# A bidirectional encoder trunk on one core: group norm per scan step, substitution in one piece, 512-column products

## The chip, the cores and the metric

The kernel runs on one core of one Trainium2 chip. The metric is the device time of one execution in microseconds (us); several executions of the same program are taken and their median is compared. All times inside the kernel come from one execution recorded by the hardware profiler.

The engines are named as in the profile: PE is the matrix engine (PEld its weight loads), DVE the vector engine, ACT the scalar engine, POOL the general engine, SP the queue from which this kernel issues its DMAs.

## What is computed

The program is two layers of an encoder on 256 tokens of width 1024, then a final norm. Every sub-layer is scaled and shifted by nine vectors that a product of the conditioning vector with `ada_w` gives.

```python
def reference(x, c, positions, ada_w, ada_b, ...):
    cs = jax.nn.silu(c)
    for l in range(DEPTH):
        mod = cs @ ada_w[l] + ada_b[l]
        sh1, sc1, gt1, sh2, sc2, gt2, sh3, sc3, gt3 = jnp.split(mod, N_MOD, axis=-1)
        h = modulate(rmsnorm(x, norm_gains[l, 0]), sh1, sc1)
        x = x + 0.5 * gt1[:, None, :] * swiglu(h, ffn_wi[l, 0], ffn_wo[l, 0])
        h = modulate(rmsnorm(x, norm_gains[l, 1]), sh2, sc2)
        x = x + gt2[:, None, :] * hybrid_mixer(h, ...)
        h = modulate(rmsnorm(x, norm_gains[l, 2]), sh3, sc3)
        x = x + 0.5 * gt3[:, None, :] * swiglu(h, ffn_wi[l, 1], ffn_wo[l, 1])
    return rmsnorm(x, final_norm)
```

`swiglu` is a product with `ffn_wi` (1024 to 2 x 2816), a gate, and a product with `ffn_wo` (2816 to 1024). The mixer has three branches on one input projection: A and B are attentions, C is a recurrent scan (RWKV-7) that runs once forwards and once backwards, followed by a group norm per head:

```python
    _, ys = lax.scan(_rwkv_step, init, (tm(r), tm(decay), tm(k), tm(v), tm(-kk), tm(kk * a)))
    y = _flip_bwd(jnp.moveaxis(ys, 0, 2))
    mean = jnp.mean(y, axis=-1, keepdims=True)
    var = jnp.mean(jnp.square(y - mean), axis=-1, keepdims=True)
    yn = ((y - mean) * lax.rsqrt(var + GN_EPS)).reshape(2, B, S, C) * gn_w + gn_b
    ...
    return (jnp.sum(yn + bonus, axis=0) * g).astype(pr.dtype)
```

The three branch outputs are each multiplied by a gate and a branch matrix, added, and multiplied by `w_out`.

## The kernel before

**Dense products.** Activations lie with channels on the 128 partitions and the 256 tokens along the free axis. Each fp32 weight tile and each fp32 activation is split into a rounded part (hi) and the rest (lo). Weights come in by DMA as pieces of 128x1024 (`wraw`); ACT casts a 128x512 quarter to `whi` (L374), DVE subtracts it for `wlo` (L383). A ring of four such quarters (`NSPL`) feeds PE. For each 128x128 tile PE makes three matmuls of 256 columns, in `mm3`: whi with hi (L418), whi with lo (L419), wlo with hi (L420). `dense` runs `mm3` over the tiles of one output block.

**Feed-forward, second product.** 22 gated tiles `z` times `ffn_wo`, 8 output blocks `m`, in four feed-forwards: 704 weight tiles. `residual` (L609) then adds the PSUM block, scaled by the gate vector, to the residual `xT` on DVE; the next norm's work follows from it.

**The scan (branch C).** The 256 tokens are four chunks of 64. In step n the forward direction takes chunk n and the backward direction chunk 3-n, both in the same instructions. For each n, `invert` inverts a triangular matrix for all 16 heads: it starts with 8x8 blocks in `blocks8` (gathering the blocks, then a forward substitution of seven steps, two small DVE operations in each, L1288 and L1292, each of which needs the one before), spreads the result (L1295), transposes it (`flip`, L1300), and then joins blocks with matmuls `pX` and `pT`. `values` prepares the values, and `scan` makes the step: `pAS`, `pU`, `pS`, `pY`. Two threads of `invert` take (0, 2) and (1, 3); two chunks' buffers are there (`s_ck`), and a step frees one when its `pY` has been copied. One buffer of values is there (`s_vl`), freed at the same point.

**Group norm.** `post(d, t)` works on one direction and one half of the tokens (two chunks): squares on ACT, sums by matmul (`pvar`), square root on ACT, reciprocal on DVE, transposes (`pgi`), then products with the gate `G1` and sums with the other direction's result and the bonus `bon`. The halves are complete after step 1 (two of the four) and after step 3 (the other two). The last two write the branch's output `oC` (hi by ACT L1516, lo by DVE L1518), on which the branch matrix of C waits. `y` is kept in the place of the values.

**The order of the work** is written out when the program is built. Each piece of work is a thread; `yield on(engine, time, latency)` says which engine the next instructions occupy and for how long by estimate, `wait` and `take` are events and buffers. A planner (`Order.run`) always takes the thread that can start first, by priority (the lower number first) where several can start at the same time, and so fixes the order of instructions on each engine. The engines run that order as it stands. `weights_lo` has priority -1, `residual` and evacuations 0 to 2, `invert`, `scan` and `post` 3, `values` 4, the bonus (`finish`) 6, the dense stream 7, the reduction of `ada_w` (L482, `araw`) 9.

## Time and profile before

| what | value |
|---|---|
| median of 3 runs | 1536.39 us (1534.38 to 1541.68) |
| the profiled execution, its own time | 1537.14 us |
| its span, first to last instruction | 1535.3 us |
| mean granted TensorE clock | 0.99 |
| PE busy | 1495.0 us (97%) |
| PEld busy | 1424.6 us (93%) |
| DVE busy | 1283.9 us (84%) |
| ACT busy | 859.4 us (56%) |
| DMA | 315.76 MB, mean 206 GB/s |

How to read it: busy time is the time in which an engine has an instruction under way; PE's instructions overlap, and the pace of a stream is read from the starts of its instructions. The granted clock is the share of full speed at which PE was clocked in a stretch: 1.00 is 2.4 GHz and 0.50 is 1.2 GHz. In rows, `out<-in` names the tiles that an instruction writes and reads, L418 is line 418 of the kernel, and brackets give the idle time before an instruction and what ended it.

### The profile page before, as it was taken

The page shows a single profiled execution, that of the slowest core. Times are in us where ns is not written, and L with a number is a line of the kernel's source. Part 1 is how long each engine was busy: PE and PEld are TensorE (multiplying, and loading weights), DVE is VectorE, ACT ScalarE, POOL GpSimd, SP SyncE. Part 2 cuts the span into 40 slices and gives each one's busy share as a digit, 9 for nine tenths or more (in the row PEclk, how much of TensorE's full clock was granted, in tenths as well). Part 3 has the DMA queues.
Part 4 walks back from the last instruction along what each step waited for, and adds up shares of the span by engine and source line. Part 5 has one row for each costly group of instructions (what it writes and reads, how often), then busy time and mean ns, then how long its engine had stood idle before and what let it go on. Part 6 is the DMA issues. An engine that isn't in the chain of part 4 may idle for free.

```text
span 1535.3 us, 36372 instructions
## 1 busy us (share of the span) xinstructions
PE 1495.0 (97%) x14470; PEld 1424.6 (93%) x14470; DVE 1283.9 (84%) x2731; ACT 859.4 (56%) x1735; POOL 2.3 (0%) x22
## 2 busy tenths in 40 slices
PE   6999999999999989999999999999999998999998
PEld 6999999988888979999999999998888998999997
DVE  8889789989878888988789877899897888898664
ACT  4556466575444447555565545676655445665554
POOL 0000000000000000000000000000000000000000
PEclk9999999999999979999999999999999999999999
DMA  9688775525345645888668886644343456567553
GB/s 343 226 293 277 259 239 188 179 102 172 118 153 166 211 165 188 280 286 271 223 201 273 276 271 222 216 159 161 109 149 102 167 207 234 167 212 267 189 183 124
DMA packets 97377, 315.76 MB, mean 206 GB/s; under 512 B 11572, under 2 KB 23092, under 8 KB 97208
## 3 DMA queue, kind: packets, MB, share of 16 engines
q1 hardware_dynamic: 96920, 313.35, 60.8%
q8 instruction: 113, 1.85, 0.5%
q14 instruction: 56, 0.46, 0.1%
q10 hardware_dynamic: 288, 0.10, 0.0%
HBM read 310.27 MB, written 3.15 MB: 204 GB/s over the span
## 4 chain that ended last, share of the span: by engine, by line
PE 89%; DMA 5%; DVE 3%; issue 1%; SPq 1%; ACT 0%; DVEq 0%; ACTq 0%
PE pmain L418 21%; PE pmain L419 20%; PE pmain L420 20%; DMA araw<-in_ada_w_dram 3%; PE pearly L418 3%; PE pearly L420 2%; PE pearly L419 2%; DVE wlo L383 1%; PE pT L1225 1%; PE pX L1213 1%; PE pS L1568 1%; PE po L1608 1%; PE pfirst L419 1%; PE pmain L1724 1%; PE pfirst L420 1%; PE pfirst L418 1%
## 5 line engine op out<-in xcount | busy, mean ns | idle before, releaser
L374 ACT CAST whi<-wraw 128x512 fp32r<-128x512 f32 x828 | 508.1, 619 | 444.8 <-PE pmain L419 283.2
L383 DVE TENSOR_TENSOR wlo<-wraw,whi 128x512 fp32r<-128x512 f32 x828 | 567.1, 689 | 117.5 <-ACT whi L374 107.8
L418 PE MATMUL pmain<-h,whi 128*128 128x256 f32 x1840 | 530.5, 288 | 0.0
L419 PE MATMUL pmain<-h,whi 128*128 128x256 f32 x1840 | 517.6, 281 | 0.0
L420 PE MATMUL pmain<-h,wlo 128*128 128x256 f32 x1840 | 515.2, 280 | 0.6 <-DVE wlo L383 0.5
L418 PEld LDWEIGHTS pmain<-h,whi 128*128 128x128 f32 x1840 | 345.9, 188 | 13.9 <-issue 7.8
L420 PEld LDWEIGHTS pmain<-h,wlo 128*128 128x128 f32 x1840 | 347.2, 189 | 1.6 <-DVE wlo L383 1.4
L419 PEld LDWEIGHTS pmain<-h,whi 128*128 128x128 f32 x1840 | 346.5, 188 | 1.1 <-issue 0.7
L482 DVE CUSTOM_DVE_ANT_0 araw<-araw,csb 128x1024 f32<-128x1024 f32 x144 | 175.5, 1221 | 47.2 <-DMA araw<-in_ada_w_dram 46.9
L420 PE MATMUL pmain<-z,wlo 128*128 128x256 f32 x704 | 199.1, 283 | 5.6 <-DVE wlo L383 5.6
L419 PE MATMUL pmain<-z,whi 128*128 128x256 f32 x704 | 198.9, 282 | 0.0
L418 PE MATMUL pmain<-z,whi 128*128 128x256 f32 x704 | 198.1, 281 | 0.0
L420 PEld LDWEIGHTS pmain<-z,wlo 128*128 128x128 f32 x704 | 133.3, 189 | 6.8 <-DVE wlo L383 6.8
L418 PEld LDWEIGHTS pmain<-z,whi 128*128 128x128 f32 x704 | 133.3, 189 | 0.0
L419 PEld LDWEIGHTS pmain<-z,whi 128*128 128x128 f32 x704 | 133.3, 189 | 0.0
L418 PE MATMUL pearly<-xh,whi 128*128 128x258 f32 x320 | 91.4, 286 | 0.0
L419 PE MATMUL pearly<-xl,whi 128*128 128x258 f32 x320 | 90.4, 283 | 0.0
L420 PE MATMUL pearly<-xh,wlo 128*128 128x258 f32 x320 | 90.4, 282 | 0.0
L419 PEld LDWEIGHTS pearly<-xl,whi 128*128 128x128 f32 x320 | 60.6, 189 | 0.0
L420 PEld LDWEIGHTS pearly<-xh,wlo 128*128 128x128 f32 x320 | 60.5, 189 | 0.0
L418 PEld LDWEIGHTS pearly<-xh,whi 128*128 128x128 f32 x320 | 60.4, 189 | 0.0
L441 ACT CAST z<-ffz 128x256 fp32r<-128x256 f32 x76 | 30.6, 405 | 39.8 <-DVE ffz L673 39.7
(308 smaller groups left out, 2328.3 us busy)
## 6 DMA issues: line engine op xcount, KB each, us to landing
wraw<-in_ffn_wi_dram SPq DMA_DIRECT2D x160, 512.0 KB, 4.7
araw<-in_ada_w_dram SPq DMA_DIRECT2D x144, 512.0 KB, 6.5
wraw<-in_ffn_wo_dram SPq DMA_DIRECT2D x88, 512.0 KB, 4.6
wraw<-in_w_in_dram SPq DMA_DIRECT2D x78, 512.0 KB, 3.7
wraw<-in_w_gb_dram SPq DMA_DIRECT2D x72, 512.0 KB, 4.0
w0raw<-in_ffn_wi_dram SPq DMA_DIRECT2D x16, 512.0 KB, 10.9
wraw<-in_w_out_dram SPq DMA_DIRECT2D x16, 512.0 KB, 3.7
bt<-in_bt_dram SPq DMA_DIRECT2D x16, 192.0 KB, 4.4
```

The source lines that it names most:

```text
L374: S_.copy(hi, part(q))
L383: V.tensor_tensor(lo, part(q), hi, op=OP.subtract)
L418: P.matmul(o, w[0], xh, start=first, stop=False)
L419: P.matmul(o, w[0], xl, start=False, stop=False)
L420: P.matmul(o, w[1], xh, start=False, stop=last)
L441: S_.copy(self.hi(k), src)
L482: V.tensor_tensor_reduce(out=raw, in0=raw, in1=csb, scale=0.5, scalar=0.0, op0=OP.mult, op1=OP.add, accum_out=modT[l][:, blk:blk + 1])
L1213: P.matmul(px[half(h), d, h // 2], G[h % 2][half(h), d, h // 2, 0:64], T[half(h), d, h // 2], start=True, stop=True)
L1225: P.matmul(pt[half(h), d, h // 2], X[half(h), d, h // 2], TT[half(h), d, h // 2], start=True, stop=True)
L1568: P.matmul(pS[e][:, t], qT[half(e), hp, t * 128:(t + 1) * 128], kT[half(e), hp], start=True, stop=True)
L1608: P.matmul(po[half(e)], vv[:, j, (2 * hp + e) * 64:(2 * hp + e + 1) * 64], pr_[:, 2 * e + j], start=j == 0, stop=j == 1)
L1724: P.matmul(p[t], ha.hi(kk)[:, xs], wh, start=kk == 0, stop=False)
```

## The change

Four things are changed.

First, the blocks of the second feed-forward product keep hi and lo of a tile side by side (`Pairs`), and `dense2` makes one matmul of 512 columns with whi (both hi and lo at once, into the two halves of the PSUM bank) and one of 256 columns with wlo. `residual2` adds the second half of the bank to `xT` with an instruction of its own before `residual` adds the first.

Second, `blocks8` gives the planner one entry for its five gathering operations (2.54) and one for the whole substitution, the spreading and the transposition (3.2), where it gave 4 and 16 entries. The instructions are the same.

Third, the group norm runs once per step, `post(n)`, on both directions' chunks of that step (64 tokens each). Steps 0 and 1 add to `bon`, steps 2 and 3 write `oC`.

Fourth, `y` and the squares lie in the step's own tile (`W1`, `TT`), so a step's `pY` is copied by one operation, the tile is freed by `post`, and two tiles of the values are freed earlier.

```diff
+    def dense2(p, a, kt):
+        for k in range(kt):
...
+            P.matmul(p, tl.last[0], a.both(k), start=k == 0, stop=False)
+            P.matmul(p[:, 0:256], tl.last[1], a.hi(k), start=False, stop=k == kt - 1)
             tl.done()
...
+    def residual2(m, p, g, st):
+        yield on("DVE", 0.4, 0.0)
+        V.scalar_tensor_tensor(xT[:, m], p[:, 1], g[:, m:m + 1], xT[:, m], op0=OP.mult, op1=OP.add)
+        yield from residual(m, p[:, 0], g, st)
...
-            yield from dense(p[:, 0], za, NJ)
-            od.spawn(residual(m, p[:, 0], g, nst), 1)
+            yield from dense2(p.rearrange("p a b -> p (a b)"), za, NJ)
+            od.spawn(residual2(m, p, g, nst), 1)
...
                 yield from blocks8(G, X, TT)
-                yield on("DVE", 0.6)
                 flip(T, TT)
...
+            yield on("DVE", 3.2)
             for i in range(7):
                 k, t0, t1 = 7 - i, slice(i + 1, 8), slice(0, 7 - i)
-                yield on("DVE", 0.13, 0.13)
                 V.tensor_mul(up[:, :, :, 0:k], skew(lb[:, 0, :, t0, i], lb[:, 1, :, t1, k]),
...
-                yield on("DVE", 0.13, 0.13)
                 c = skew(tc8[:, 0, :, t0], tc8[:, 1, :, t1])
                 V.tensor_add(c, c, up[:, :, :, 0:k])
             od.release(s_px)
-            yield on("DVE", 0.6)
             V.tensor_mul(by_k(TT), flat(tc8)[:, :, None, :].to_broadcast([128, 8, 8, 8]),
...
-                for d in range(2):
-                    yield from copy_any(RKV[d, 2][:, :, toks(cs[d])], p[:, d], 256)
-                    if n % 2 == 1:
-                        od.set(e_y[d, cs[d] // 2])
+                YS[n] = (W1, TT)
+                yield from copy_any(W1, p, 512)
                 od.release(s_px)
-                free_big(5 - (n == 3))
+                od.set(e_y[n])
+                free_big(4 - (n == 3))
...
-        def post(d, t):
+        def post(n):
-            last = d != t
-            ts = slice(t * 128, (t + 1) * 128)
-            yield wait(e_y[d, t])
-            y = RKV[d, 2][:, :, ts]
+            last = n > 1
+            ts = [toks(n), toks(3 - n)]
+            both = lambda t: skew(t[:, :, ts[0]], t[:, :, ts[1]])
+            yield wait(e_y[n])
+            y, sq = YS[n]
...
-            for d in range(2):
-                for t in range(2):
-                    od.spawn(post(d, t), 3)
+            for n in range(4):
+                od.spawn(post(n), 3)
```

## Rows read from the trace of the kernel before

**Rows 1.** The page's first part: busy us, share of the span, instructions of each engine.
```profile
PE 1495.0 (97%) x14470; PEld 1424.6 (93%) x14470; DVE 1283.9 (84%) x2731; ACT 859.4 (56%) x1735; POOL 2.3 (0%) x22
```
**Rows 2.** Waits of PE: engine, tile, line, releaser: us in total, times, longest.
```profile
PE pmain L420 <- DVE wlo L383: 6.1, 6, 2.3
PE pmain L418 <- ACT oC L1516: 5.5, 3, 3.4
```
**Rows 3.** Timeline of PE, end of layer 0's scan: start us, us, instruction, idle before.
```profile
536.91 1.15 PE L1409 MATMUL pY<-ar,st 64*64 64x64 f32 x32
...
539.05 0.28 PE L420 MATMUL pmain<-o,wlo 128*128 128x256 f32 x1
...
550.11 0.58 PE L418 MATMUL pmain<-oC,whi 128*128 128x256 f32 x1 [3.40 <-ACT oC L1516]
...
553.28 0.58 PE L419 MATMUL pmain<-oC,whi 128*128 128x256 f32 x1 [0.46 <-DVE oC L1518]
```
**Rows 4.** Windows: us, then busy us (count) of PE, PEld, DVE, ACT, POOL; clock; DMA.
```profile
540.00:550.00 10.00, 3.41 (x20) 2.83 (x19) 7.79 (x19) 2.85 (x6) 0.00 (x0) 0.58 0.74 270
550.00:560.00 10.00, 9.31 (x43) 8.43 (x44) 7.38 (x19) 3.54 (x8) 0.00 (x0) 0.57 0.01 4
...
1290.00:1300.00 10.00, 6.63 (x49) 5.70 (x47) 8.83 (x22) 6.76 (x13) 0.00 (x0) 0.96 0.80 283
1300.00:1310.00 10.00, 8.59 (x52) 8.29 (x53) 9.11 (x22) 3.45 (x7) 0.00 (x0) 0.69 0.51 161
```
**Rows 5.** Timeline of PE at the end of layer 1's scan.
```profile
1281.70 1.15 PE L1409 MATMUL pY<-ar,st 64*64 64x64 f32 x32
...
1285.37 1.84 PE L1471 MATMUL pvar<-c_sel,gsq 128*128 128x2 f32 x16
...
1294.22 0.28 PE L420 MATMUL pmain<-o,wlo 128*128 128x256 f32 x1
```
**Rows 6.** Substitution by line: count, ns min/median/max, first and last start us, forms.
```profile
L1288 DVE TENSOR_TENSOR w<-p,w x12: 167/184/209, 402.1 to 415.7; 128x40 f32<-128x40 f32 x2, 128x32 f32<-128x32 f32 x2, 128x24 f32<-128x24 f32 x2, 128x16 f32<-128x16 f32 x2
...
L1288 DVE TENSOR_TENSOR w<-p,w x7: 166/186/217, 489.6 to 507.5; 128x56 f32<-128x56 f32 x1, 128x48 f32<-128x48 f32 x1, 128x40 f32<-128x40 f32 x1, 128x32 f32<-128x32 f32 x1
...
L1300 DVE STREAM_TRANSPOSE tx<-tw x1: 704/704/704, 511.7 to 511.7; 128x512 f32<-128x512 f32 x1
...
L1288 DVE TENSOR_TENSOR w<-p,w x7: 161/177/216, 1230.0 to 1246.0; 128x56 f32<-128x56 f32 x1, 128x48 f32<-128x48 f32 x1, 128x40 f32<-128x40 f32 x1, 128x32 f32<-128x32 f32 x1
```
**Rows 7.** Timeline of DVE: substitution operations that stand next to one another.
```profile
1213.16 0.19 DVE L1288 TENSOR_TENSOR w<-p,w 128x32 f32<-128x32 f32 x1
...
1214.05 0.17 DVE L1288 TENSOR_TENSOR w<-p,w 128x16 f32<-128x16 f32 x1
```
**Rows 8.** Timeline of PE: second feed-forward product, then the 512-column products of V.
```profile
163.10 0.28 PE L420 MATMUL pmain<-z,wlo 128*128 128x256 f32 x1
...
165.93 0.28 PE L420 MATMUL pmain<-z,wlo 128*128 128x256 f32 x1
...
290.73 0.39 PE L1724 MATMUL pmain<-whi,h 128*128 128x512 f32 x1
...
299.76 0.40 PE L1724 MATMUL pmain<-whi,h 128*128 128x512 f32 x1
```
**Rows 9.** Group of the residual (busy us, mean ns, idle), and a second product's window.
```profile
L609 DVE SCALAR_TENSOR_TENSOR xT<-pmain,g,xT 128x256 f32<-128x256 f32 x48 | 23.1, 482 | 14.8 <-PE pmain L420 14.7
...
146.00:206.00 60.00, 56.57 (x460) 56.17 (x459) 47.27 (x88) 29.01 (x54) 0.93 (x7) 0.97 0.80 270
```
**Rows 10.** DVE beside layer 0's scan: window, `araw` group in it, one quarter's `wlo`, its use.
```profile
385.00:540.00 155.00, 154.02 (x2438) 137.74 (x2437) 131.26 (x292) 71.67 (x151) 0.00 (x0) 1.00 0.51 166
...
L482 DVE CUSTOM_DVE_ANT_0 araw<-araw,csb 128x1024 f32<-128x1024 f32 x21 | 25.6, 1217 | 1.6 <-DMA araw<-in_ada_w_dram 1.5
...
406.05 0.68 DVE L383 TENSOR_TENSOR wlo<-wraw,whi 128x512 fp32r<-128x512 f32 x1
...
409.55 0.28 PE L420 MATMUL pmain<-h,wlo 128*128 128x256 f32 x1
```

More of the change, by code (lines that the diff above doesn't have):

```diff
@@ L447, in free, with __init__, hi, lo @@
             free_big(2 * self.n)
+    class Pairs(Act):
+        def __init__(self, name, kt):
+            self.n = -(-kt // 4)
+            self.t = [big(name, (128, 2, 2, S), F32R) for _ in range(-(-kt // 2))]
+            self.ev = [Event() for _ in range(kt)]
+        def hi(self, k):
+            return self.t[k // 2][:, k % 2, 0]
+        def lo(self, k):
+            return self.t[k // 2][:, k % 2, 1]
+        def both(self, k):
+            return self.t[k // 2][:, k % 2].rearrange("p a b -> p (a b)")
+        def free(self):
+            free_big(len(self.t))
     class Early:
@@ L469, in dense @@
             mm3(p, tl.last, a.hi(k), a.lo(k), k == 0, k == kt - 1)
+            tl.done()
+    def dense2(p, a, kt):
+        for k in range(kt):
+            yield from tl.next()
+            if a.ev[k].t is None or a.ev[k].t > od.cur.t:
+                yield wait(a.ev[k])
+            yield on("PE", MM, 0.0)
+            P.matmul(p, tl.last[0], a.both(k), start=k == 0, stop=False)
+            P.matmul(p[:, 0:256], tl.last[1], a.hi(k), start=False, stop=k == kt - 1)
             tl.done()
@@ L763, in first_products @@
             if k == KT - 1:
-                yield take(s_big, 12)
-                za = Act("z", NJ)
+                yield take(s_big, 11)
+                za = Pairs("z", NJ)
             for i in range(NJ0 // 2):
@@ L795, in ffn @@
             od.spawn(modulated(l, n, st, ha), 0)
-            yield take(s_big, 12)
-            za = Act("z", NJ)
+            yield take(s_big, 11)
+            za = Pairs("z", NJ)
         for j in range(j0, NJ):
@@ L1293, in blocks8 @@
             od.release(s_px)
-            yield on("DVE", 0.6)
             V.tensor_mul(by_k(TT), flat(tc8)[:, :, None, :].to_broadcast([128, 8, 8, 8]),
@@ L1347, in values @@
             if n_val[0] == 4:
-                free_big(4)
-        e_y = {(d, t): Event() for d in range(2) for t in range(2)}
+                free_big(6)
+        e_y, YS = [Event() for _ in range(4)], {}
         def scan():
@@ L1452, in gating @@
             od.set(e_gate)
-        def post(d, t):
-            last = d != t
-            ts = slice(t * 128, (t + 1) * 128)
-            yield wait(e_y[d, t])
-            y = RKV[d, 2][:, :, ts]
-            yield take(s_z2)
-            sq = small2("gsq", (128, 4, 128))
+        def post(n):
[4 more added lines that the diff above has]
+            y, sq = YS[n]
+            sqt = sq.rearrange("p d h t -> p (d h t)").rearrange("p (h d t) -> p h d t", h=4, d=2)
             yield on("ACT", 0.48)
-            S_.activation(sq, y, AF.Square)
-            if WARM:
-                yield on("ACT", 0.094, tab="sqrt")
-                S_.activation(warm, eps_r, AF.Sqrt)
+            S_.activation(sqt.rearrange("p h d t -> p d h t"), y, AF.Square)
+            flat = sqt.rearrange("p h d t -> p h (d t)")
             yield take(s_px)
             p = paux("pvar", (128, 8))
-            yield on("PE", 0.8)
+            yield on("PE", 0.9)
             for hp in range(4):
-                P.matmul(p[:, 2 * hp:2 * hp + 2], sq[:, hp], sel[:, 0, 0:2], start=True, stop=True)
+                P.matmul(p[:, 2 * hp:2 * hp + 2], flat[:, hp], sel[:, 0, 0:2], start=True, stop=True)
             yield wait(e_gate)
-            if last:
-                yield on("DVE", 0.6)
-                V.tensor_mul(y, y, G1[0][:, :, ts])
+            yield on("DVE", 0.6)
+            V.tensor_mul(y, y, both(G1[0]))
             r = tmp.tile([128, 8], F32, name="gr")
@@ L1479, in post @@
             od.release(s_px)
[L1480 removed]
+            yield on("DVE", 0.43)
             V.reciprocal(r, r)
[L1482 to L1484 removed]
+            V.tensor_copy(flat.rearrange("p a (b c) -> p (a b) c", b=2), r[:, :, None].to_broadcast([128, 8, 64]))
             yield take(s_px)
[L1486 to L1487 removed]
+            p = paux("pgi", (128, 4, 2, 64))
+            yield on("PE", 0.5)
             for hp in range(4):
[L1489 to L1491 removed]
+                P.transpose(p[:, hp].rearrange("p d t -> p (d t)"), flat[:, hp], ident)
+            pd = p.rearrange("p h d t -> p d h t")
+            b = both(bon[0])
             if not last:
[L1493 to L1494 removed]
+                yield on("DVE", 1.2)
+                V.tensor_mul(y, y, pd)
+                V.tensor_add(b, b, y)
                 od.release(s_px)
[L1496 to L1500 removed]
+                od.set(e_z[n])
             else:
@@ L1507, in post @@
                 yield wait(e_oC)
-                yield wait(e_z[t])
+                yield wait(e_z[3 - n])
+                h, lo = both(oC[0].h[0]), both(oC[0].l[0])
                 for q in range(2):
                     sl = slice(2 * q, 2 * q + 2)
-                    yield on("DVE", 0.335)
-                    V.tensor_mul(y[:, sl], y[:, sl], p[:, sl])
-                    yield on("DVE", 0.335)
-                    V.tensor_add(y[:, sl], y[:, sl], b[:, sl])
-                    yield on("ACT", 0.264)
-                    S_.copy(oC[0].h[0][:, sl, ts], y[:, sl])
-                    yield on("DVE", 0.335)
-                    V.tensor_tensor(oC[0].l[0][:, sl, ts], y[:, sl], oC[0].h[0][:, sl, ts], op=OP.subtract)
+                    yield on("DVE", 0.67)
+                    V.tensor_mul(y[:, :, sl], y[:, :, sl], pd[:, :, sl])
+                    V.tensor_add(y[:, :, sl], y[:, :, sl], b[:, :, sl])
+                    yield on("ACT", 0.264)
+                    S_.copy(h[:, :, sl], y[:, :, sl])
+                    yield on("DVE", 0.335)
+                    V.tensor_tensor(lo[:, :, sl], y[:, :, sl], h[:, :, sl], op=OP.subtract)
                     for k in range(2 * q, 2 * q + 2):
```

22 lines of the change are left out of this document (3 added, 19 removed).

## The prediction

> **What bounds the kernel now.** I read the page's busy times first: PE is busy 97% of the span, so the time is PE's stream plus what interrupts it [rows 1]. Second the list of PE's waits: it is short, and its large entries are the branch output `oC` at the end of the scans and `wlo` in the second feed-forward products [rows 2]. Third the timeline and the windows at the end of the two scans [rows 3 to 5]. In layer 0 the last `pY` runs from 536.91, the last dense matmul that needs nothing of the scan starts at 539.05, and then PE has only the group norm's small matmuls until `oC` arrives: first part at 550.11, second at 553.28 [rows 3]. The granted clock is 0.58 and 0.57 in these two windows (full speed falls to half, 1.2 GHz, and comes back only after the dense stream has run for some us) [rows 4]. In layer 1 dense work lasts until 1294.22, and the same hole follows, smaller [rows 4, 5].
>
> The price of the two holes: a dense matmul of 256 columns starts every 2.83 / 24 = 0.118 us at full clock [rows 8], a `pvar` matmul every 1.84 / 16 = 0.115 [rows 5]; I take 0.115 for `pgi` too. From 540 to 560 PE started 63 instructions, 20 small and 43 dense: 20 x 0.115 + 43 x 0.118 = 7.4 us of work in 20, so 12.6 us lost. From 1290 to 1310 it started 101, 8 of them small: 0.9 + 93 x 0.118 = 11.9 in 20, so 8.1 lost [rows 4]. Together 20.7 us, the most that moving the scan can bring.
>
> **Substitution in one piece.** The same 14 small operations, spreading and transposition; what changes is who may stand between them. In step 3 of layer 0 the seven products start from 489.6 to 507.5 and the transposition at 511.7 (+0.70): 22.8 us [rows 6]. Where the operations stand next to one another they start (1214.05 - 1213.16) / 4 = 0.22 us apart [rows 7], so a piece costs 14 x 0.22 + 0.7 (spreading, as long as the transposition) + 0.7 = 4.5 us, and this inversion ends 18 us sooner. Steps 0 and 1 run interleaved, 12 of their 14 products within 402.1 to 415.7 [rows 6]; two pieces of 4.5 there save some 5 us, and step 1 stands ahead of step 3 in the chain (it frees step 3's buffers). Layer 1's step 3 has products from 1230.0 to 1246.0 alone [rows 6], against 4.5 for the whole piece. So the end of the scan moves forward by up to 18 + 5 = 23 us; at least 0, because the bonus, the one buffer of values, and PE's queue stand in the same chain and may take over. I take 15, nearer to the row of step 3, since that inversion is last in the chain.
>
> Here a rule speaks against the change. The Trainium skill, "VectorE: DVE Perf Modes", Rules for kernel authors, says not to fuse chained operations for speed because every operation empties the pipe anyway, and to lower their number instead. By that rule, with the number unchanged, this edit brings nothing and the chain stays as it is: that is the first rival below. The rows speak for a gain of another kind: 22.8 us for 4.5 us of operations is waiting in the queue, which the rule does not treat.
>
> **What the piece costs.** For 4.5 us DVE does nothing else, eight times in all. Queued behind it are `wlo` (PE waits for that), residuals of other branches, and the other steps of the scan. The cover is the ring of split weights: the shortest lead I found there is a `wlo` that ended at 406.73 and was first used at 409.55, 2.8 us ahead [rows 10]. At that lead a piece stops PE for 1.7 us, at the usual longer ones for nothing. Bounds 0 and 8 x 1.7 = 14 us; I take 3, as the short leads are few. The gathering in one piece holds DVE for less than the substitution, under the same cover: nothing on top.
>
> **Group norm by step.** Half of the work that now follows the last `pY` moves to step 2: one square, 8 of 16 `pvar`, one product with the gate, half of the transposes, 6 of the 12 DVE operations on 128x256. DVE operations of this size take 0.4 to 0.5 us (as L609, rows 9), so this is 6 x 0.4 + 8 x 0.115 + about 1.7 for square and gate product = 5 us. The second part of `oC` stood 553.28 - 538.06 = 15.2 us behind the end of `pY` [rows 3]; it becomes 10. Layer 0's hole closes when the scan ends 538.06 + 10 - 539.3 = 9 us earlier; 15 is more. In layer 1 `pY` ends at 1282.85 and dense work lasts to 1294.5 [rows 5]: 10 us fit without any help from the substitution. More switches of ACT's table (square root per step) fall on an engine busy 71.67 of 155 us [rows 10] and are hidden by that; if they were not, `whi` would be late within the same lead. Fewer, larger copies of `y` and the buffers freed earlier: nothing.
>
> **512 columns.** A tile took three matmuls at 0.118. The V products are of 512 columns with a weight load before each: 39 intervals from 290.73 to 299.76, 0.2315 each [rows 8]. A tile then costs 0.2315 + 0.118 = 0.3495 against 0.3538: 0.0043 x 704 = 3.0 us. Bounds: 0, and 704 x 0.034 = 24 if a tile cost only its columns (768 at 2.4 GHz, 0.320 us); I take 3.0, by the row of the very shape. The `residual2` operation, 32 x 0.48 = 15 us of DVE [rows 9], lies beside PE where DVE is busy 47.27 of 60 us [rows 9]: nothing, except behind the last matmul of the program, where 0.4 us are added. If that cover is gone, a `wlo` wait as in [rows 2] lengthens by up to 0.5 us per block.
>
> **Sum**, against the execution's own 1537.1: - 20.7 - 3.0 + 0.4 + 3 = 1516.8; the median of the runs is 0.7 lower than this execution, so 1516. With its own bounds (lead cost 0 to 8, 512 columns 0 to 8) this case spans 1507 to 1524.
>
> **Rivals.**
> *The chain does not get shorter* (bonus or values take over, as the rule above would also have it). Then layer 1 still closes by the shorter group norm (8.1), layer 0 gains 4 or 5 of its hole: 1537.1 - 8.1 - 4.5 - 3.0 + 0.4 + 3 - 0.7 = 1524. For it: several waits stand in that chain. Against it: 18 us in one inversion.
> *The hole moves.* DVE has 155 - 131.26 = 24 us free beside layer 0's scan, and 21 reductions of `araw`, 25.6 us, are the lowest in rank there [rows 10]. If the tail's DVE work, 7.8 us between 540 and 550 [rows 4], now falls before 540, a third of that room is gone; where it was not free at the right moments, the reductions slip behind, and the gate vector of the mixer's output waits for them. Half of the two holes comes back: 1516 + 10 + 4 = 1530.
> *Slower: DVE's pieces drain the ring.* Each of eight pieces stops PE for its full 4.5 us if the lead is gone when it starts: 36 instead of 3, 1549. It decides against the change from 3 us per piece on (24 us gained over eight), that is at a mean lead under 1.5 us. Against it: 2.8 was the shortest seen.
> *Loads set PE's pace.* The Trainium skill, "Perfetto Trace Analysis", Identifying the Most-Contended Engine, judges PE's headroom by the busy share of its weight loads; by it the loads, a third fewer here, would be worth more than the columns. PEld is busy 93% [rows 1], which would fit. By the rows this mechanism gives a tile of bare columns, 24 instead of 3 us: 1495. Against it: the V products have one load per 512 columns, time to spare for it, and still start every 0.2315 us instead of 0.213.
>
> **Chances.** Forecast 0.66, chain not shorter 0.14, hole moves 0.10, slower 0.06, loads 0.04. A measurement here tells about 0.5% from no change, that is below 1528.7 for faster: forecast, first rival and the last give 0.84; the moved hole is within 0.5%, 0.10; slower 0.06. The range 1507 to 1532 holds the forecast's own span, the first rival and the moved hole.
>
> **What would show it.** Right: no PE wait on `oC`, a granted clock of 1.00 through both scan ends, L1288 to L1300 of a step within some 5 us, the last `pY` of layer 0 some 15 us before the dense work runs out, 0.35 us per tile of `z`. Wrong: waits of PE on `wlo` or on `tx` (L1300) inside the scans, each after a piece; a new wait at the mixer's output product; 512-column matmuls that start at another pace than 0.23 us.

## The result and the profile after

The changed kernel takes 1519.9 us (median of four runs, 1518.35 to 1520.62), the kernel before 1536.1 in the same session: ratio 0.9894, 95% interval 0.988 to 0.9907, some 16 us. The profiled execution of the changed kernel took 1520.03 us, its span is 1517.9 (1535.3 before), the mean granted clock 0.996.

The page's first part, for [rows 1]: PE has 14 us less to do and fills 98% of a shorter span, DVE has 22 us more and is at 86%.

```profile
PE 1481.0 (98%) x13766; PEld 1383.0 (91%) x13766; DVE 1305.7 (86%) x2771; ACT 865.2 (57%) x1727; POOL 2.3 (0%) x22
```

The waits of PE, for [rows 2] (engine, tile, line, releaser: us in total, times, longest). The wait for `oC` is gone. `wlo` is still there, `tx` (L1331, the transposition behind a piece) has grown from 0.7 us in one place, and `m` is new (the merged sum in front of the output product).

```profile
PE pmain L500 <- DVE wlo L383: 4.6, 3, 3.1
...
PE pX L1248 <- DVE tx L1331: 3.5, 7, 0.7
...
PE pmain L420 <- DVE wlo L383: 3.0, 3, 1.6
...
PE pmain L419 <- DVE m L443: 1.6, 2, 0.9
```

The timeline of PE at the end of layer 0's scan, for [rows 3]: the last `pY` begins 19.5 us earlier than before, and the branch matrix of C follows the dense stream at its pace, 0.11 us behind the matmul ahead of it.

```profile
517.40 1.15 PE L1440 MATMUL pY<-ar,st 64*64 64x64 f32 x32
...
541.79 0.28 PE L420 MATMUL pmain<-o,wlo 128*128 128x256 f32 x1
541.90 0.28 PE L418 MATMUL pmain<-oC,whi 128*128 128x256 f32 x1
```

The windows of [rows 4], same columns (us, then busy us and count of PE, PEld, DVE, ACT, POOL; clock; DMA). The clock is 1.00 in all four, where it was 0.57 to 0.96. Another column has moved as much: DVE, which was busy 7.4 to 9.1 of 10 us in the holes, is now busy 9.5 to 10.

```profile
540.00:550.00 10.00, 10.00 (x87) 10.00 (x86) 9.48 (x22) 5.30 (x10) 0.00 (x0) 1.00 0.87 308
550.00:560.00 10.00, 9.22 (x78) 9.02 (x77) 10.00 (x28) 4.97 (x10) 0.00 (x0) 1.00 0.69 259
1290.00:1300.00 10.00, 9.79 (x83) 9.58 (x81) 10.00 (x27) 5.74 (x13) 0.00 (x0) 1.00 0.83 299
1300.00:1310.00 10.00, 8.36 (x68) 8.16 (x69) 9.90 (x26) 5.83 (x13) 0.00 (x0) 1.00 0.37 124
```

**Where the time went**, from the first and last starts of each stage's matmuls in the two traces:

| stage | layer | before, us | after, us | difference |
|---|---|---|---|---|
| end of the first feed-forward to the end of the branch matrix of C | 0 | 351.1 | 337.7 | -13.4 |
| same | 1 | 344.7 | 336.5 | -8.2 |
| mixer's output product (`m`) | 0 | 22.9 | 27.1 | +4.2 |
| same | 1 | 22.9 | 25.3 | +2.4 |
| four second products `z` | both | 258.5 | 253.6 | -4.9 |
| all the rest | both | 535.2 | 537.8 | +2.6 |
| span (parts rounded) | | 1535.3 | 1517.9 | -17.4 |

The holes are closed, and the output product right behind each of them has become longer. The windows show how: the branch matrix of C (first and third line) and the output product (second and fourth).

```profile
541.90:553.20 11.30, 11.30 (x98) 11.30 (x97) 11.17 (x27) 5.94 (x11) 0.00 (x0) 1.00 0.88 312
553.20:580.20 27.00, 24.58 (x194) 24.17 (x192) 25.25 (x59) 16.91 (x34) 0.00 (x0) 0.94 0.51 176
1282.80:1294.10 11.30, 11.30 (x98) 11.30 (x97) 11.30 (x27) 6.57 (x13) 0.00 (x0) 1.00 0.93 330
1294.10:1319.40 25.30, 23.44 (x195) 23.04 (x194) 24.82 (x59) 16.04 (x35) 0.00 (x0) 1.00 0.54 195
```

At PE's full speed DVE is the fuller engine here. Its timeline gives the time from start to start of each operation: 0.34 us for `mgd`, 0.60 for `wlo`, 0.33 for `sg`, 0.33 for the low part of `m`, together 1.60 us for one of the eight output blocks. PE needs 12 x 0.118 = 1.42 us for a block.

```profile
544.24 0.42 DVE L1795 TENSOR_TENSOR mgd<-mgd,sg 128x256 f32<-128x256 f32 x1
544.58 0.68 DVE L383 TENSOR_TENSOR wlo<-wraw,whi 128x512 fp32r<-128x512 f32 x1
545.18 0.41 DVE L1791 SCALAR_TENSOR_TENSOR sg<-sg,pmain 128x256 f32<-128x256 f32 x1
545.51 0.68 DVE L383 TENSOR_TENSOR wlo<-wraw,whi 128x512 fp32r<-128x512 f32 x1
...
548.96 0.42 DVE L443 TENSOR_TENSOR m<-mgd,m 128x256 fp32r<-128x256 f32 x1
549.29 0.74 DVE L1791 SCALAR_TENSOR_TENSOR sg<-sg,pmain 128x256 f32<-128x256 f32 x2
```

What DVE has not done by 553 falls into the output product, and two reductions of `ada_w` stand in the same queue, in front of the `wlo` that PE waits for. First DVE, then PE:

```profile
557.94 1.21 DVE L513 CUSTOM_DVE_ANT_0 araw<-araw,csb 128x1024 f32<-128x1024 f32 x1
...
559.42 1.21 DVE L513 CUSTOM_DVE_ANT_0 araw<-araw,csb 128x1024 f32<-128x1024 f32 x1
```

```profile
559.55 0.39 PE L419 MATMUL pmain<-m,whi 128*128 128x256 f32 x1 [0.78 <-DVE m L443]
...
561.94 0.38 PE L420 MATMUL pmain<-m,wlo 128*128 128x256 f32 x1 [1.64 <-DVE wlo L383]
```

After these two waits the granted clock is at half for 3.4 us, which costs 1.7 (the 0.94 of the window: 27 x 0.06 = 1.6). 0.78 + 1.64 + 1.7 = 4.1 is layer 0's +4.2. In layer 1 the same two waits are 0.85 and 1.0 us and the clock stays at 1.00.

The second product `z`, by line (busy us, mean ns of one, idle before). The median step from L499 to L500 is 0.232 us and from L500 to L499 0.118, over all 704 tiles.

```profile
L499 PE MATMUL pmain<-z,whi 128*128 128x512 f32 x704 | 248.7, 396 | 0.0
L500 PE MATMUL pmain<-z,wlo 128*128 128x256 f32 x704 | 199.0, 283 | 4.6 <-DVE wlo L383 4.6
```

The substitution of step 3 in layer 0, on the timeline of DVE, for [rows 6]: first product to end of the transposition 481.54 to 486.16, 4.6 us where it took 22.8, with nothing in between.

```profile
481.54 0.22 DVE L1321 TENSOR_TENSOR w<-p,w 128x56 f32<-128x56 f32 x1
...
484.52 0.17 DVE L1324 TENSOR_TENSOR w<-w 128x8 f32<-128x8 f32 x1
...
485.45 0.71 DVE L1331 STREAM_TRANSPOSE tx<-tw 128x512 f32<-128x512 f32 x1
```

### The profile page after: what moved, and what is told of

The parts are those of the page before. It is cut to its first block, busy times and chain, and to the rows that moved or that the text cites. A ratio compares the mean times of both kernels' runs of the same rounds, so it can differ in the third digit from the quotient of the medians.

```text
span 1517.9 us, 35002 instructions
## 1 busy us (share of the span) xinstructions
PE 1481.0 (98%) x13766; PEld 1383.0 (91%) x13766; DVE 1305.7 (86%) x2771; ACT 865.2 (57%) x1727; POOL 2.3 (0%) x22
## 4 chain that ended last, share of the span: by engine, by line
PE 88%; DVE 7%; DMA 2%; issue 1%; ACT 0%; SPq 0%; DVEq 0%; ACTq 0%
PE pmain L418 16%; PE pmain L419 15%; PE pmain L420 15%; PE pmain L499 10%; PE pmain L500 5%; PE pearly L419 2%; PE pearly L418 2%; PE pearly L420 2%; DVE wlo L383 2%; PE pS L1591 1%; PE pfirst L419 1%; PE pmain L1746 1%; PE pPT L1622 1%; PE pfirst L420 1%; PE pX L1248 1%
## 5 line engine op out<-in xcount | busy, mean ns | idle before, releaser
L499 PE MATMUL pmain<-z,whi 128*128 128x512 f32 x704 | 248.7, 396 | 0.0
L500 PE MATMUL pmain<-z,wlo 128*128 128x256 f32 x704 | 199.0, 283 | 4.6 <-DVE wlo L383 4.6
L499 PEld LDWEIGHTS pmain<-z,whi 128*128 128x128 f32 x704 | 132.9, 189 | 30.9
L500 PEld LDWEIGHTS pmain<-z,wlo 128*128 128x128 f32 x704 | 133.1, 189 | 5.8 <-DVE wlo L383 5.8
L441 ACT CAST z<-ffz 128x256 fp32r<-128x256 f32 x76 | 30.6, 405 | 29.7 <-DVE ffz L709 29.5
L418 PE MATMUL pfirst<-h,w0h 128*128 128x256 f32 x128 | 36.9, 288 | 3.1 <-ACT h L781 3.1
L420 PE MATMUL pmain<-m,wlo 128*128 128x256 f32 x128 | 36.8, 287 | 2.6 <-DVE wlo L383 2.6
```

Source lines behind the costliest of these rows:

```text
L418: P.matmul(o, w[0], xh, start=first, stop=False)
L420: P.matmul(o, w[1], xh, start=False, stop=last)
L441: S_.copy(self.hi(k), src)
L499: P.matmul(p, tl.last[0], a.both(k), start=k == 0, stop=False)
L500: P.matmul(p[:, 0:256], tl.last[1], a.hi(k), start=False, stop=k == kt - 1)
```

## The experiments

The kernels come in three groups: the parts of the change alone, the parts of the changed kernel taken back or altered, and the size of what DVE still owes at the output product. Ratios are against the kernel before in the same session. The start of "the last `pY`" is from here on that of its last matmul (537.8 us before, 518.3 after, in layer 0). "Tail" is the time from there to the start of the last operation that writes the low part of `oC`; it is 15.0 us in layer 0 and 18.9 in layer 1 before, 16.8 and 16.2 after.

The theory at the start was that of the prediction: the parts fill the holes each for itself, so they add. Its rival: they do not add, because a sooner scan end and a shorter tail are needed together.

### The piece alone

The kernel before with the planner's entries of the changed `blocks8`.

```diff
+            yield on("DVE", 2.54)
...
-                yield on("DVE", 0.6, 0.0)
...
+            yield on("DVE", 3.2)
...
-                yield on("DVE", 0.13, 0.13)
...
-                yield on("DVE", 0.13, 0.13)
```

> The kernel before with the gathering and the substitution in one piece each, nothing else of the change. Theory (the scan ends sooner and the two holes behind it are filled): the last pY of layer 0 ends near 519 instead of 538, that of layer 1 some 16 us sooner; PE no longer waits for oC in layer 0; of 20.7 us some 4 us come back as PE waits on tx inside the scans and some 6 as waits in the mixer's output product, so 1523 to 1529 us. Rival (only the shorter group norm closes the holes): the last pY hardly moves or the hole stays, 1533 us or more.

Measured: 1541.2 us, ratio 1.0029 (1.0019 to 1.0039). The last `pY` of layer 0 begins 26.9 us sooner (510.9 for 537.8) and that of layer 1 16 us, of which 9.8 come from before that layer's mixer and 6.2 are its own; so the piece does what it says. But the tails grow to 28 us in layer 0 and 32 in layer 1. PE's waits, the first in layer 0 and the other two in layer 1:

```profile
PE pearly L418 <- DVE xh L547: 3.5, 1, 3.5
PE pmain L418 <- ACT oC L1511: 3.5, 1, 3.5
...
PE pS L1385 <- DVE uv L1375: 3.1, 1, 3.1
```

The timeline of DVE in layer 1 shows the tail. Each operation of the old group norm is an entry of its own with a latency behind it, and in that gap go a `wlo`, a merge, and even a reduction of the lowest priority:

```profile
1289.03 0.42 DVE L1509 TENSOR_TENSOR rkv<-rkv,bon 128x256 f32<-128x256 f32 x1
1289.36 1.22 DVE L482 CUSTOM_DVE_ANT_0 araw<-araw,csb 128x1024 f32<-128x1024 f32 x1
...
1296.55 0.42 DVE L1507 TENSOR_TENSOR rkv<-rkv,pgi 128x256 f32<-128x256 f32 x1
1296.88 1.22 DVE L482 CUSTOM_DVE_ANT_0 araw<-araw,csb 128x1024 f32<-128x1024 f32 x1
...
1298.91 0.43 DVE L1513 TENSOR_TENSOR oC<-rkv,oC 128x256 fp32r<-128x256 f32 x1 [0.47 <-ACT oC L1511]
```

Before, this tail ran in the hole, with no dense work beside it; now it queues with dense work, as the substitution did. Layer 0's hole closed all the same: the dense work behind the scan lasts until `oC` is needed, 29.7 us after the last `pY`, and the tail is 28.3. The stretch from the first feed-forward to the end of the branch matrix takes 337.8 us there, as in the full change (337.7). Then PE waits 3.5 us for `xh` (the next norm's first block), with the late reductions ahead of it on DVE. In layer 1 the tail of 32.3 us is longer than the dense work, and the stretch takes 352.2 us for 344.7; the wait for `uv` is part of that (DVE stood 4.88 us for the data of `bt` ahead of it). The profiled execution, 1535.2 us, is the shortest of ten; the other nine took 1539.7 to 1542.7. Where those lose their further 4 to 7 us is not shown.

### The group norm by step alone

The kernel before with the new `post(n)`, the step's own tile for `y`, and the old `blocks8`.

```diff
+        def post(n):
-        def post(d, t):
...
+            for n in range(4):
+                od.spawn(post(n), 3)
```

> The kernel before with the group norm step by step, nothing else. Theory: the last pY stays where it was (538 and 1283 us), the tail behind it is 5 us shorter; layer 1's hole (8.1) closes nearly, layer 0's goes from 12.6 to about 8; with 2 to 3 us of new waits in the output product 1526 to 1531 us. Rival (only the earlier end of the scan counts): 1533 us or more.

Measured: 1539.2 us, ratio 1.0013 (1.0004 to 1.0023). The tails are 10.5 and 13 us, as short as forecast, but the last `pY` begins 5.2 and 5.6 us later than before: the group norm of steps 0 to 2 now stands at the scan's own priority between the scan's operations. That this is what delays the scan is argued from the order, not shown. And at the end of layer 0 DVE, with lower-ranked reductions ahead in its fixed order, stood idle 1.93 us for the data of one of them; the group norm's product with the gate (L1471), whose input ACT was done with at 544.56, came only at 546.80:

```profile
545.64 1.23 DVE L482 CUSTOM_DVE_ANT_0 araw<-araw,csb 128x1024 f32<-128x1024 f32 x1 [1.93 <-DMA araw<-in_ada_w_dram]
...
546.80 0.69 DVE L1471 TENSOR_TENSOR tw<-tw,g 128x512 f32<-128x512 f32 x1
```

### The 512 columns alone

The kernel before with `Pairs`, `dense2` and `residual2`.

```diff
+            yield from dense2(p.rearrange("p a b -> p (a b)"), za, NJ)
+            od.spawn(residual2(m, p, g, nst), 1)
-            yield from dense(p[:, 0], za, NJ)
-            od.spawn(residual(m, p[:, 0], g, nst), 1)
```

> The kernel before with the 512-column products and the second residual operation, nothing else. Theory: 0.0043 us per tile, 704 tiles, less 0.4 at the end: 1533.4 us, at 0.232 and 0.118 us from start to start. Rival (loads set the pace): a tile costs 0.320, 1512 us. Rival (the added DVE operation delays wlo): 1536 us or more, with longer waits of PE on wlo in the second products.

Measured: 1532.1 us, ratio 0.9977 (0.9961 to 0.9993), 3.5 us with an interval of 1.1 to 6.0. This part stands by itself, and its term in the sum (3.0 less 0.4) lies well inside.

### The change without the piece

```diff
-            yield on("DVE", 3.2)
...
+                yield on("DVE", 0.13, 0.13)
...
+                yield on("DVE", 0.13, 0.13)
```

> The changed kernel with the old entries for gathering and substitution, that is group norm by step and 512 columns without the piece. Theory: sum of the two alone, 1523 to 1528 us, so the piece is worth 4 to 8 us on top of the others, with a wait for oC left in layer 0 and none on tx. Rival (the piece brings nothing once the group norm is short): 1520 us, as the changed kernel.

Measured: 1539.3 us, ratio 1.0015 (1.0004 to 1.0025). The tails are the shortest of all, 8.6 and 10.6 us, and the last `pY` the latest, 5.9 and 11.4 us later than before. The holes are as deep as ever, in layer 1 too:

```profile
540.00:550.00 10.00, 6.01 (x76) 5.09 (x75) 5.53 (x13) 3.05 (x5) 0.00 (x0) 0.67 0.42 168
...
1290.00:1300.00 10.00, 5.24 (x72) 4.66 (x72) 4.57 (x10) 3.17 (x5) 0.00 (x0) 0.67 0.54 210
```

So with 512 columns worth 3.5, the piece alone costs 4.5 us, the group norm alone 2, the two together bring some 13. The parts do not add; the theory of the prediction falls here. The theory that took its place: a hole closes when the tail, at the length that it has beside full-rate dense work, ends before that dense work does; so the scan has to end sooner and the tail's operations have to stand together in the order. Its rival: what counts in the new group norm is that half of its work has left the tail.

### The changed kernel with the tail's entries taken apart again

```diff
...
-                    yield on("DVE", 0.67)
+                    yield on("DVE", 0.335)
                     V.tensor_mul(y[:, :, sl], y[:, :, sl], pd[:, :, sl])
+                    yield on("DVE", 0.335)
                     V.tensor_add(y[:, :, sl], y[:, :, sl], b[:, :, sl])
```

> The changed kernel with the group norm's pairs of operations given to the planner one by one again (product and sum in the last steps, reciprocal and spreading), instructions unchanged. Theory (the tail behind the last pY is short because its operations stand together, and single entries let wlo, merges and araw in between): the last oC part comes 3 to 8 us later in each layer (17 and 16 us behind the last pY now), and PE waits for oC or loses clock again in at least one layer: 1525 to 1532. Rival (half the work behind the last pY is what counts, not the grouping): within 2 us of 1520.

Measured: 1525.8 us, ratio 0.9950 (0.9931 to 0.9969), against 0.9894 for the changed kernel: 8.6 us by the ratios. With the same instructions the tails are 25 and 28 us for 16.8 and 16.2, and the wait for `oC` is back:

```profile
PE pmain L418 <- ACT oC L1541: 1.9, 1, 1.9
PE pmain L419 <- DVE oC L1543: 1.4, 1, 1.4
```

### The piece, with the old tail's entries grouped

The kernel of the piece alone, with the same grouping in the old `post(d, t)`.

```diff
...
-                    yield on("DVE", 0.335)
+                    yield on("DVE", 0.67)
                     V.tensor_mul(y[:, sl], y[:, sl], p[:, sl])
-                    yield on("DVE", 0.335)
                     V.tensor_add(y[:, sl], y[:, sl], b[:, sl])
```

> The kernel before with the substitution in one piece (as e1) and the old group norm's pairs of operations (product and sum of the last step, reciprocal and spreading) grouped for the planner, instructions unchanged. Theory (the piece alone gave nothing because the old group norm's single entries queue behind wlo, merges and araw once dense work runs beside them, 28 and 32 us from the last pY to the last part of oC; grouping took 9 and 12 us off that in the changed kernel): the tail falls to 18 to 22 us in both layers, layer 1's wait for oC (3.4 us) and its 6.8 us of half clock go: 1528 to 1535. Rival (half of the work having left the tail is what the changed kernel needs): the tail stays at 25 us and more, 1539 to 1543.

Measured: 1535.5 us, ratio 0.9994 (0.9984 to 1.0004), 5.4 us better than the piece alone by the ratios, and half a microsecond above the theory's range. The tails are 17.6 and 21.5 us, the wait for `oC` is gone, and both ends run at full clock. The window of layer 1:

```profile
1290.00:1300.00 10.00, 10.00 (x87) 10.00 (x86) 9.63 (x20) 5.32 (x10) 0.00 (x0) 1.00 0.96 341
```

In layer 0 the stretch from the first feed-forward to the end of the branch matrix takes 338.4 us, 337.7 in the full change and 337.8 with the piece alone: there the piece is all that is needed, and neither the grouping nor half of the work leaving the tail is. In layer 1 it takes 344.9, no less than before and 8.4 more than in the full change, although its hole is closed too: PE waited 3.3 us for `uv` near 1172, where DVE stood 5.14 us for the data of `bt` (L1554), and had half clock for 3.4 us behind that, which costs 1.7. The other 3.4 us are not traced to a cause. So piece and grouping together only come back to the time before; by the ratios 15 us separate this kernel from the changed one, and without the 3.5 of the 512 columns some 12 of them come with the group norm by step. Which of its effects brings them (less work in the tail, buffers freed earlier, or an order without such accidents) is not shown.

### What lengthens the output product

Two causes were to be told apart: DVE is full while the branch matrix of C runs, or the two reductions in front of `wlo` are to blame. Two kernels keep the order of every engine and only shorten operations; they leave work out, and so measure its price and nothing else.

The four reductions, 8 columns of 1024:

```diff
+        w = 8 if blk in (54, 55) else D
-        V.tensor_tensor_reduce(out=raw, in0=raw, in1=csb, scale=0.5, ...
+        V.tensor_tensor_reduce(out=raw[:, 0:w], in0=raw[:, 0:w], in1=csb[:, 0:w], scale=0.5, ...
```

> The changed kernel in the same order on every engine; the last two reductions of ada_w of each mixer (the two that stand beside the mixer's output product) read 8 columns of 1024, so that most of their 1.2 us is left out. Theory of the araw reductions (these four, 4.4 us of DVE time in all, make the extra of 4.3 and 2.4 us at the output product): PE's waits at the output product go or fall below 0.5 us, the half clock in layer 0 goes, output products of 23 us: 1513 to 1516. Rival (the backlog of a full DVE is longer than that, and two reductions less only shorten it): waits fall by about half, 1517 to 1519.

The 16 additions of branch C, 8 columns of 256:

```diff
+                w = 8 if b == 2 else S
-                V.tensor_add(g, g, s)
+                V.tensor_add(g[:, 0:w], g[:, 0:w], s[:, 0:w])
```

> The changed kernel in the same order on every engine; the 16 additions of branch C's product into the merged sum work on 8 columns of 256, so that most of their time (0.33 us from start to start) is left out. Theory of the full DVE (its work while the branch matrix of C runs is longer than PE's, and the rest falls into the output product): 8 x 0.25 = 2.0 us a layer less, so PE's waits of 2.4 and 1.9 us at the output product fall below 0.6 and the half clock goes: 1513 to 1516. Rival (only the two araw reductions count): waits stay within 0.8 us of what they were, 1518 to 1521.

Measured: 1516.0 us (ratio 0.9865, 0.9848 to 0.9882) and 1518.3 (0.9879, 0.9862 to 0.9896). The output products, first with short reductions, then with short additions:

```profile
552.60:576.70 24.10, 23.32 (x194) 22.71 (x193) 23.59 (x61) 16.16 (x35) 0.00 (x0) 1.00 0.62 210
...
1292.80:1316.30 23.50, 23.46 (x193) 22.93 (x192) 22.96 (x60) 15.98 (x36) 0.00 (x0) 1.00 0.62 215
```

```profile
552.90:577.10 24.20, 22.75 (x193) 22.55 (x192) 23.62 (x59) 15.86 (x34) 0.00 (x0) 1.00 0.60 198
...
1293.30:1317.00 23.70, 23.10 (x194) 22.90 (x193) 23.03 (x57) 15.41 (x34) 0.00 (x0) 1.00 0.62 210
```

Either edit takes some 2 us from DVE in each layer, and either takes 2.8 or 2.9 us from the output product of layer 0 and 1.6 to 1.8 from that of layer 1, half clock included. So it is neither the one nor the other by itself but one queue: DVE's backlog, whatever it is made of. This rests on the output products of one trace each; the ratios of the whole program overlap that of the changed kernel (0.9880 to 0.9907). Both theories missed in part: with short reductions the output products stay above the 23 us expected, and with short additions 1.45 us of a wait for `wlo` stay, which was expected below 0.6. Part of the gain is lost again in layer 0's second feed-forward product, which takes 64.3 and 64.9 us in these two for 61.8 in the changed kernel; with short reductions DVE stood there 3.12 us for the data of another reduction, and PE 1.35 for the `wlo` behind it.

### The additions on GpSimd

The same 16 additions, moved instead of shortened.

```diff
+                if b == 2:
+                    yield on("POOL", 0.7, 0.15)
+                    nc.gpsimd.tensor_add(g, g, s)
```

> The changed kernel, with the addition of branch C's product into the merged sum (mgd, 8 blocks a layer, 0.33 us each on DVE) given to GpSimd. Theory (DVE is full while the branch matrix of C runs, 11.2 of 11.3 us, and what is left over falls into the output product): 8 x 0.33 = 2.6 us a layer leave DVE just there, so most of the output product's extra (27.0 and 25.2 us instead of some 22.8) goes: 1516 us, and no wait of PE for wlo or m between 553 and 580. Rival (the two araw reductions that stand ahead of wlo make the extra, however full DVE is): within 1 us of 1520.

Measured: 1521.8 us, ratio 0.9917 (0.9903 to 0.9932); output products of 27.3 and 28.0 us: neither what the theory nor what the rival gave. The load did not leave DVE: its window over the branch matrix (first line) has 22 operations instead of 27 and is as full as before. One addition takes GpSimd 1.13 us in the mean (last line), and while it runs DVE's `wlo` takes 1.26 instead of 0.69 and the low part of `m` 0.96 instead of 0.42.

```profile
541.20:552.50 11.30, 11.30 (x99) 11.30 (x98) 11.13 (x22) 5.87 (x11) 4.68 (x5) 1.00 0.91 311
```

```profile
544.73 1.26 DVE L383 TENSOR_TENSOR wlo<-wraw,whi 128x512 fp32r<-128x512 f32 x1 [0.17 <-ACT whi L374]
...
547.60 0.96 DVE L443 TENSOR_TENSOR m<-mgd,m 128x256 fp32r<-128x256 f32 x1
...
550.89 0.41 DVE L1791 SCALAR_TENSOR_TENSOR sg<-sg,pmain 128x256 f32<-128x256 f32 x1
```

```profile
550.45 2.26 POOL L1796 TENSOR_TENSOR mgd<-mgd,sg 128x256 f32<-128x256 f32 x2 [2.17 <-DVE sg L1791]
```

```profile
L1796 POOL TENSOR_TENSOR mgd<-mgd,sg 128x256 f32<-128x256 f32 x16 | 17.9, 1129 | 793.6 <-DVE sg L1791 406.9 <-ACT whi L374 386.0 <-PE pmain L419 0.8
```

`sg`, which reads one operand from PSUM, keeps its 0.41 beside GpSimd's additions (they run from 550.45). So this run does not decide between the two causes; the two above do.

### The reductions earlier

Loads and reductions of `ada_w` for the mixer start earlier in the planner's time: 150 for 190, then 165 with 4.2 for 4.5 us between two.

```diff
-PACE, START = 4.5, 190
+PACE, START = 4.5, 150
```

> The changed kernel, with the loads and reductions of ada_w for the mixer starting 40 us earlier in the planner's time (150 for 190), so that the last reductions fall before the branch matrix of C. Theory of the araw reductions (1.2 us each, two of them beside the oC product of each layer): without them in the backlog PE's waits of 2.4 us in layer 0 and 1.9 in layer 1 at the output product go, with 1.7 us of half clock: 1514 to 1516. Rival (full DVE): the same work has to be done elsewhere in the scan, and the output product stays at 27 and 25 us: 1519 to 1522. The order of everything in the scan can shift by this too; which it was is to be read from the output product's length, not from the total.

```diff
-PACE, START = 4.5, 190
+PACE, START = 4.2, 165
```

> The changed kernel with the loads of ada_w for the mixer starting at 165 instead of 190 and every 4.2 instead of 4.5 us, at which the fixed order has no reduction beside the output product in either layer, and as much dense work (192 matmuls) between the last pY and the branch matrix of C. Theory: output products of 22.5 us in both layers, as in e6, and no hole: 1512 to 1516 if the scans stay as long as in the changed kernel. Rival (the reductions cost as much beside the start of the scan as beside the output product, as in e6): output products of 22.5 us, and the scans longer by 7 us or more: 1520 to 1527.

Measured: 1527.0 us (0.9952, 0.9934 to 0.9970) and 1519.4 (0.9888, 0.9872 to 0.9904). No reduction stands beside the output products any more, and these take what PE needs: 22.4 and 22.5 us, then 22.5 and 22.7 (here the second kernel, layer 0):

```profile
555.30:577.80 22.50, 22.50 (x194) 22.50 (x193) 21.78 (x53) 16.06 (x33) 0.00 (x0) 1.00 0.58 188
```

The scans pay: up to the end of the branch matrix 346.4 and 346.4 us with the first setting, 340.6 and 343.4 with the second, for 337.7 and 336.5. In the first, PE is busy 5.3 us of 10 near the start of layer 0's scan, with DVE full, where the changed kernel has 9.57 and 8.43:

```profile
420.00:430.00 10.00, 5.31 (x105) 3.84 (x104) 9.96 (x30) 5.10 (x18) 0.00 (x0) 0.93 0.51 172
```

Only two of the 24 reductions of a mixer run in this window, and the order of everything else differs too; so it is not shown that the moved reductions are what lengthens the scans. As far as the runs go: out of the output product's way they give back all of its extra, and no kernel that moves them is faster as a whole.

### The planner told a longer piece

The substitution takes 4.6 us where its entry says 3.2, the gathering 3.3 where its entry says 2.54.

```diff
-            yield on("DVE", 2.54)
+            yield on("DVE", 3.2)
...
-            yield on("DVE", 3.2)
+            yield on("DVE", 4.4)
```

> The changed kernel with the planner told a longer time for the two pieces (3.2 and 4.4 us where it has 2.54 and 3.2), so that the matmul that needs a piece's result is placed later in PE's fixed order. Theory (PE waits for tx, 3.5 us in seven places and the small ones beside it, because the piece takes longer than its entry says and PE cannot pass the waiting matmul): the waits of PE on tx fall below 1 us and the total by 2 to 4 us, to 1517. Rival (the waits are the chain's own and only move): tx waits gone but the last pY later by as much, 1520.

Measured: 1528.6 us, ratio 0.9958 (0.9943 to 0.9974): missed in the other direction. The order came out differently throughout the scans, PE's waits for the substitution rose, and the last `pY` came 4.6 and 18.6 us later:

```profile
PE pX L1293 <- DVE tx L1331: 5.3, 3, 2.2
...
PE pX L1248 <- DVE w L1321: 4.8, 2, 2.4
```

A truer time for one entry does not make a better order here; what the waits for `tx` would give back is left open.

No kernel run here computes the whole reference faster than the changed one by more than the intervals.

## Why the prediction came out as it did

The forecast was 1516, measured were 1519.9 by the median and 1520.0 in the profiled execution, inside the range and in the forecast's own case. The total is right for reasons that are only partly those given, and in part by luck: the two ends of the scans brought 3.9 us more and the second products 1.9 us more than the sum has, which makes up for 5.8 of the 8.8 us that the sum lacks (6.6 at the output product, 2.2 elsewhere). The span that it states for its own case, 1507 to 1524, takes 0 to 8 us for the pieces and for the columns, where the text above it gives 0 to 14 and 0 to 24; with those bounds it would have been 1492 to 1530.

**The holes: price about right, reason incomplete.** The 20.7 us for the two holes, less 3 for the pieces, stand against 21.6 measured up to the end of the two branch matrices (13.4 and 8.2). Closed they are: no wait for `oC`, clock 1.00, as listed under what would show it. But the text let each part close a hole for itself: 15 us of a sooner scan end in layer 0, and in layer 1 "10 us fit without any help from the substitution". For layer 0 the trace of the piece alone bears it out, up to the end of the branch matrix. For layer 1 the runs refute it. Without the piece it keeps its hole although the tail is as short as forecast (10.6 us), because the last `pY` comes 11.4 us later: the half of the group norm that moves in front of that `pY` was put at nothing there. With the piece alone layer 1's tail is longer than its dense work, and over the whole program nothing is gained.

**The failed step: the tail was taken as a fixed length.** It was to fall from 15.2 to 10 us by what leaves it. Where PE is idle it does (10.5 and 8.6 us in layer 0 without the piece). In the changed kernel it is 16.8, because it now runs beside dense work and shares DVE with `wlo` and merges; with single entries it is 25. What I saw in the substitution (22.8 us for 4.5 us of operations, waiting in the queue) holds for every chain of small operations that a change moves out of an idle stretch into a full one, and I did not apply it to the very tail that I was moving. That its operations stand together is worth 8.6 us by the ratios in the changed kernel, and 5.4 with the old group norm, and the prediction counted it nowhere.

**The missed term: 6.6 us at the output product.** [rows 4] showed DVE busy 7.4 to 9.1 of 10 us in the holes. I read the holes as lost time; for DVE they were not. It worked off its queue there (the tail and three reductions of `araw`, in layer 0), and when PE runs through at full speed that work is still to be done. The rival of the moved hole named the mechanism (the reductions slip behind, the output product waits) at 0.10 and 14 us; it came true at 6.6, on top of the forecast and not instead of it. It should have stood in the sum as a bounded cost. Worked out afterwards as an estimate: DVE's 1.60 us for a block against PE's 1.42 make 2.9 us over 16 blocks, and four reductions of 1.14 us from start to start 4.6 more.

**The pieces: size about right, place wrong.** The forecast had PE stopped by a drained ring (3 us). No wait for `wlo` lies inside the scans; PE waits for the piece's own result `tx`, 3.5 us in seven places, as the signs listed, since its fixed order puts `pX` too early. The sooner scan end, 23 us at most and 15 taken, was 19.5 in layer 0; in layer 1, counted from the end of the feed-forward ahead of it, it was 15.7.

**512 columns: right.** 0.232 + 0.118 us for a tile, as worked out from [rows 8]; 3.5 us alone (1.1 to 6.0), 4.9 in the stage table of the full change, where 3.0 are the tile's and the rest is not separated. The rival of the loads (24 us) falls: a third fewer loads in these products did not change the step of 0.232 us. The Trainium skill, "Perfetto Trace Analysis", Identifying the Most-Contended Engine, judges PE's headroom by MFU (its FLOPs against the peak) or by the busy share of its weight loads. That share does not tell here whether loads or columns set the pace: it was 93% before and is 91% with a third fewer loads in these products, while a tile went from 0.354 to 0.350 us only.

**The rule on chained operations.** The first rival leaned on the Trainium skill, "VectorE: DVE Perf Modes", Rules for kernel authors. As a statement on the operations themselves it stands: from the first to the last of the 14 there are 2.98 us, 0.23 from start to start, no less than before [rows 7]. As a forecast of the time it gives 1524 and misses, since the time between the operations was the cost. That the piece alone was worth nothing (1.0029) is not for the rule's reason.

**Nothing for the rest** was nearly right: 2.6 us, of which 1.0 at the program's end, where 0.4 were put for the second residual operation.

## What to carry to other kernels

Before you count an idle stretch of the bound engine as gain, look what the other engines do in it: work that they finish there has to be done elsewhere once the stretch is gone, and it is a term of the sum. A chain of small operations that is moved beside full-rate work gets as long as the queue it stands in, however short its instructions; keep its operations together in a fixed order, and take its new length from a row where it runs in such company. Where two edits remove the same wait, run each alone: here both alone lose, and together they bring most of the gain.

## What the runs showed of the hardware

Two things that I had not expected.

DVE operations with two SBUF inputs do not run at full pace beside a GpSimd addition. While GpSimd's addition of two 128x256 tiles ran (1.13 us mean, 0.42 for the same on DVE), DVE operations with two SBUF inputs took 1.26 instead of 0.69 us and 0.96 instead of 0.42, and the one with an operand in PSUM stayed at 0.41. The Trainium skill, "SBUF — State Buffer", section SBUF: two separate sides, has the rule for this: a DVE operation with two SBUF inputs and a GpSimd operation that reads SBUF take an exclusive lock, and the later one waits for the whole instruction. The trace agrees: the extra 0.57 and 0.54 us are within what is left of GpSimd's addition when each begins (0.71 and 0.68, spans on GpSimd being rough).

An engine whose order is fixed passes on the wait of any one operation. DVE stood 1.93, 3.12 and 5.14 us for DMA data of `araw` or `bt` in the runs above, with the group norm, `wlo` or the scan behind it; in the last two PE waited 1.35 and 3.3 us in turn. In the changed kernel's first feed-forward the longest wait for `wlo`, 3.1 us, lies behind an `araw` that waited 2.9 for its data. The low priority of a reduction protects nobody once it stands in the order.
